# Batched matmul bound by its DMA queue: stores issued two at a time behind the loads of two groups, instead of one behind the loads of each group

## The chip, the cores and the metric

One core of a Trainium2 chip. The metric is the device time of one execution in microseconds, as the median of several runs. A program on one core has no second die to compare with, so the state of a single run can't always be told; all runs quoted here count as fast.

## The reference

```python
b1, b2, m, k, n = 8, 16, 256, 512, 384        # float32
def reference(x, weight):                      # (8,16,256,512) @ (8,16,512,384)
    return np.matmul(x, weight).astype(np.float32)
```

128 independent products. Per execution 167.8 MB are read and 50.3 MB are written.

## The kernel before

The batches go in 32 groups of four. Per group SP issues two weight loads (w, 1.57 MB each), one x load (2.10 MB) and, for an older group, one store (1.57 MB). VectorE casts w, ScalarE casts x and copies the products out of PSUM, TensorE makes 16 transposes and then 128 small matmuls. All DMAs go out from SP, so they form one queue on each of the 16 DMA engines.

```python
G, NG, T = 4, 32, 4            # batches in a group, groups, quarters of a group
XS, WS, OS = 2, 4, 4           # buffers of x_sb, w_sb, out_sb
LAG = 4
# ... cut
def load(e, t, U, s):                                     # group n = t * U + s
    for d in range(G // D):
        # waits until VectorE has cast what was in this w_sb slot (group n - 2)
        e.dma_start(w_sb[slot][:], ...).then_inc(w_in[slot], 16)
    # waits until ScalarE has cast x of group n - 2
    e.dma_start(x_sb[s % XS][:], ...).then_inc(x_in[s % XS], 16)

def store(e, t, U, s, pieces=1):
    # waits until ScalarE has copied group n out of PSUM
    e.dma_start(out=dram[:, rows], in_=out_sb[s % OS][:, rows]).then_inc(o_out[s % OS], 16)

def copy_out(e, t, U, s, q):
    if q == 0:
        # waits until store n - 4 has landed
    e.copy(out=out_sb[s % OS][:, 2 * q : 2 * q + 2, :], in_=po[...][:, :, :N])

def on_sync(e):
    U = OS
    for n in range(LAG):
        load(e, 0, NG, n)
    rounds = (NG - LAG) // U
    with e.Fori(0, rounds) as t:
        for s in range(U):
            load(e, t, U, LAG + s)
            store(e, t, U, s)
    for n in range(rounds * U, NG):          # the last four stores
        # ... cut
        store(e, 0, NG, n, T if n == NG - 1 else 1)
```

## Time and profile before

| | before |
|---|---|
| median | 518.28 us, 3 runs (518.17 to 518.58) |
| DMA queue | 218.11 MB, 99.3% of 16 engines' span |
| busiest compute engine | VectorE, 64% |
| landing of the last x load, first and last of 16 engines | 493.16 and 496.55 us |

A transfer lands on an engine when that engine raises the transfer's semaphore. The chart, the queue, the waits of SP and the windows of this kernel stand in the prediction. This is TensorE in order of time, around one group in mid-kernel (start us, length us, engine, line, what, count):

```profile
338.11 3.96 PE L166 MATMUL pt<-identity,x_bf 128*128 128x128 f32 x16 [5.47 <-ACT x_bf L132]
342.00 6.42 PE L180 MATMUL po<-w_bf,x_t 128*32 128x384 bf16 x128
```

The x load of this group landed on its last engine at 336.82 us. So TensorE's dense stretch (128 matmuls, each with a weight load) begins some 5 us after a group's x has landed; the store that stands next in the queue takes 3.6 us and is over by then. The other view is the end of the span, in windows of 5 us; the last two columns are the busy share of the DMA engines and GB/s:

```profile
500.00:505.00 5.00, 5.00 (x96) 3.52 (x99) 2.02 (x3) 2.02 (x3) 0.00 (x0) 0.88 1.01 428
505.00:510.00 5.00, 1.87 (x48) 1.01 (x40) 0.00 (x0) 1.72 (x3) 0.00 (x0) 1.00 0.98 409
510.00:515.00 5.00, 0.00 (x0) 0.00 (x0) 0.00 (x0) 0.00 (x0) 0.00 (x0) 0.64 0.44 177
```

The 16 engines don't finish together: in the last window some are done and others still write.

### The profile page before, as it was taken

What the parts mean: (1) busy time and instruction counts of PE and PEld (TensorE: products, weight loads), DVE (VectorE), ACT (ScalarE), POOL (GpSimd) and SP (SyncE); (2) the same over time, 40 slices, a digit from 0 to 9 for tenths busy, and PEclk for the clock granted to TensorE, in tenths of its full rate; (3) what the DMA queues carried; (4) which work ended last, traced back from release to release, by engine and by line L of the source; (5) the groups of instructions that cost most, each with busy time, mean ns of one, the idle gap of its engine ahead of it and who ended that gap; (6) DMA issues with size and microseconds to landing.
All of it is one profiled execution on the core that took longest, in us unless ns stands there. A gap on an engine that the chain in (4) does not pass through costs nothing.

```text
span 517.2 us, 11523 instructions
## 1 busy us (share of the span) xinstructions
PE 306.6 (59%) x4608; PEld 200.6 (39%) x4608; DVE 332.8 (64%) x384; ACT 236.7 (46%) x264; POOL 0.7 (0%) x6
## 2 busy tenths in 40 slices
PE   0478776556665457645577554776446765467752
PEld 0345444334443334433344332444324443244431
DVE  3698875667556676556675566855658656676550
ACT  0465564443644436435355354454444544544441
POOL 0000000000000000000000000000000000000000
PEclk9998877878777887878777778877788877778777
DMA  8999999999999999999999999999999999999996
GB/s 340 430 423 424 424 432 426 429 428 430 432 427 427 427 428 432 429 427 430 426 431 431 426 429 430 427 432 427 427 429 429 427 433 425 430 428 430 429 428 251
DMA packets 18869, 218.18 MB, mean 422 GB/s; under 512 B 2096, under 2 KB 2096, under 8 KB 2608
## 3 DMA queue, kind: packets, MB, share of 16 engines
q1 hardware_dynamic: 18864, 218.11, 99.3%
q8 instruction: 3, 0.05, 0.0%
q14 instruction: 2, 0.02, 0.0%
HBM read 167.77 MB, written 50.33 MB: 422 GB/s over the span
## 4 chain that ended last, share of the span: by engine, by line
DMA 81%; ACT 10%; PE 4%; issue 3%; ACTq 0%; SPq 0%
DMA x_sb<-in_x_dram 81%; ACT x_bf L132 9%; PE po L180 2%; PE pt L166 1%; ACTq L130 0%; ACT out_sb L194 0%; SPq L111 0%; SPq L103 0%; ACT L132 0%; ACTq L193 0%; SPq L282 0%; SPq L55 0%
## 5 line engine op out<-in xcount | busy, mean ns | idle before, releaser
L147 DVE CAST w_bf<-w_sb 64x1536 bf16<-64x1536 f32 x256 | 244.4, 955 | 47.2 <-DMA w_sb<-in_weight_dram 38.5
L166 PE MATMUL pt<-identity,x_bf 128*128 128x128 f32 x512 | 123.7, 425 | 199.3 <-ACT x_bf L132 199.1
L180 PE MATMUL po<-w_bf,x_t 128*32 128x384 bf16 x4096 | 185.1, 342 | 1.0 <-issue 1.0
L166 PEld LDWEIGHTS pt<-identity,x_bf 128*128 128x128 f32 x512 | 91.8, 216 | 232.1 <-issue 218.3
L194 ACT COPY out_sb<-po 128x768 f32<-128x768 f32 x128 | 102.2, 798 | 147.2 <-PE po L180 147.2
L153 DVE COPY x_t<-pt 128x1024 bf16<-128x1024 bf16 x128 | 88.4, 691 | 122.3 <-PE pt L166 121.8
L132 ACT CAST x_bf<-x_sb 128x1024 bf16<-128x1024 f32 x128 | 124.4, 1042 | 80.9 <-DMA x_sb<-in_x_dram 80.8
L180 PEld LDWEIGHTS po<-w_bf,x_t 128*32 128x32 bf16 x4096 | 108.8, 101 | 73.8 <-issue 14.2
L132 ACT ACT_TABLE_LOAD x8 | 10.3, 1283 | 42.9 <-DMA x_sb<-in_x_dram 42.9
masks.py:199 POOL TENSOR_SCALAR_AFFINE_SELECT identity<-identity 128x128 f32<-128x128 f32 x1 | 0.3, 292 | 0.2 <-POOL identity L200 0.2
L200 POOL MEMSET identity<- 128x128 f32 x1 | 0.2, 204 | 0.5 <-SPq L55 0.5
L271 POOL MEMSET const-bfloat16-1.0<- 128x1 bf16 x1 | 0.1, 101 | 0.0
L271 POOL MEMSET const-uint8-127<- 128x1 uint8 x1 | 0.1, 101 | 0.0
L271 POOL MEMSET const-float32-0.0<- 128x1 f32 x1 | 0.1, 98 | 0.2 <-issue 0.2
L271 POOL MEMSET const-float32-1.0<- 128x1 f32 x1 | 0.1, 98 | 0.0
## 6 DMA issues: line engine op xcount, KB each, us to landing
w_sb<-in_weight_dram SPq DMA_DIRECT2D x64, 1536.0 KB, 27.5
x_sb<-in_x_dram SPq DMA_DIRECT2D x32, 2048.0 KB, 27.5
out_dram<-out_sb SPq DMA_DIRECT2D x31, 1536.0 KB, 30.7
out_dram<-out_sb SPq DMA_DIRECT2D x4, 384.0 KB, 5.9
```

What stands on the lines that cost most here:

```text
L132: e.copy(out=x_bf[s % BS][:, rows], in_=x_sb[s % XS][:, rows].rearrange("p r (q s c) -> p r s q c", s=S, c=KO),).then_inc(x_cast, 1)
L147: e.tensor_copy(out=w_bf[(s * G + d * D + a) % WBS][h * HP : (h + 1) * HP], in_=w_sb[slot][a * HP : (a + 1) * HP, h * KO : (h + 1) * KO, : ...
L153: e.tensor_copy(out=x_t[s % TS][:, 2 * q : 2 * q + 2], in_=pt[(s * T + q) % PT][:].bitcast(bf16),).then_inc(t_copied, 1)
L166: ins = e.transpose(pt[(s * T + q) % PT][:, rr, h, :], words[:, 2 * q + rr, h :: KO // 2], identity[:],)
L180: ins = e.matmul(po[(s * T + q) % PO][mine, rr, :N], x_t[s % TS][:, 2 * q + rr, ko // 2, mine, ko % 2], w_bf[(s * G + i) % WBS][:, ko, :], ...
L194: e.copy(out=out_sb[s % OS][:, 2 * q : 2 * q + 2, :], in_=po[(s * T + q) % PO][:, :, :N],).then_inc(o_copied, 1)
L200: e.memset(identity[:], 0.0).then_inc(id_done, 1)
L271: nc = _bacc.Bacc("TRN2", target_bir_lowering=False, num_devices=1)
```

## The change

Its intent: the queue turns from loads to stores and back once for two groups rather than once for each.

```diff
-        for n in range(LAG):
+        for n in range(LAG + 1):
             load(e, 0, NG, n)
-        rounds = (NG - LAG) // U
+        store(e, 0, NG, 0)
+        load(e, 0, NG, LAG + 1)
+        store(e, 0, NG, 1)
+        store(e, 0, NG, 2)
+        first = LAG + 2
+        rounds = (NG - first) // U
         with e.Fori(0, rounds) as t:
-            for s in range(U):
-                load(e, t, U, LAG + s)
-                store(e, t, U, s)
+            for s in range(0, U, 2):
+                for a in range(2):
+                    load(e, t, U, first + s + a)
+                for a in range(2):
+                    store(e, t, U, first + s + a - LAG + 1)
(the loops over the last loads and stores, cut)
```

## The prediction

> **What bounds the kernel now.** I began with the page's chart of 40 slices and its table of DMA queues. One queue carries everything, and the DMA engines are over 90% busy in every slice but the first and the last, at 423 to 433 GB/s.
>
> ```profile
> DMA  8999999999999999999999999999999999999996
> GB/s 340 430 423 424 424 432 426 429 428 430 432 427 427 427 428 432 429 427 430 426 431 431 426 429 430 427 432 427 427 429 429 427 433 425 430 428 430 429 428 251
> q1 hardware_dynamic: 18864, 218.11, 99.3%
> ```
>
> No compute engine is near this: the busiest, VectorE, has 64% of the span. The chain that ended last is 81% the x load. So the time is bytes over rate, plus an edge at each end. The bytes don't change.
>
> Next the waits of the issuing engine (SP) and its instructions in order of time, to see whether the DMA engines ever run dry because an issue comes late.
>
> ```profile
> SPq L103 <- DVE w_bf L147: 269.5, 60, 8.6
> SPq L111 <- ACT x_bf L132: 122.5, 30, 5.6
> SPq L122 <- ACT out_sb L194: 35.5, 6, 16.2
> ...
> 205.23 4.29 SPq L103 DMA_DIRECT2D w_sb<-in_weight_dram  x2
> 213.89 0.33 SPq L111 DMA_DIRECT2D x_sb<-in_x_dram  x1
> 214.54 0.35 SPq L122 DMA_DIRECT2D out_dram<-out_sb  x1
> ...
> x_sb<-in_x_dram SPq DMA_DIRECT2D x32, 2048.0 KB, 27.5
> out_dram<-out_sb SPq DMA_DIRECT2D x31, 1536.0 KB, 30.7
> ```
>
> SP waits a lot, for casts that free w_sb and x_sb. But a load lands 27.5 us after its issue, and its own transfer takes under 5 us (2.10 MB at 429 GB/s), so some 22 us of other transfers stand ahead of it. The stores wait for their data in six places only, which lie at the end (the last group's pieces and those queued ahead of them).
>
> Third, the rate by stretch. The first group's store is issued at 46.74 us, and ring order puts it behind loads that land until about 64 us, so the first four windows are loads alone. The next three alternate one group of loads and one store. The last two begin after the last load is through on most engines: stores back to back.
>
> ```profile
> 5.00:17.00 12.00, 0.00 (x0) 0.00 (x0) 7.64 (x8) 0.00 (x0) 0.00 (x0) 1.00 1.01 429
> 17.00:29.00 12.00, 9.09 (x144) 6.21 (x144) 7.26 (x9) 7.58 (x9) 0.00 (x0) 1.00 1.00 428
> 29.00:41.00 12.00, 8.46 (x144) 5.46 (x144) 11.44 (x14) 6.98 (x9) 0.00 (x0) 1.00 1.01 427
> 41.00:53.00 12.00, 9.14 (x144) 5.93 (x144) 9.65 (x13) 7.49 (x9) 0.00 (x0) 0.86 1.01 426
> ...
> 132.00:164.00 32.00, 19.98 (x292) 13.38 (x292) 20.80 (x24) 15.63 (x19) 0.00 (x0) 0.77 1.01 428
> 200.00:264.00 64.00, 39.01 (x582) 25.39 (x584) 41.76 (x50) 29.60 (x33) 0.00 (x0) 0.79 1.01 429
> 300.00:364.00 64.00, 38.58 (x596) 25.45 (x584) 41.79 (x49) 30.44 (x35) 0.00 (x0) 0.79 1.01 429
> ...
> 497.00:500.00 3.00, 2.17 (x9) 1.73 (x10) 0.75 (x2) 3.00 (x4) 0.00 (x0) 0.50 1.01 430
> 500.00:503.00 3.00, 3.00 (x48) 2.16 (x51) 2.02 (x3) 0.55 (x1) 0.00 (x0) 0.81 1.01 430
> ```
>
> The last column is GB/s. Loads alone 426 to 429, alternating 428 to 429, stores alone 430. Changing direction twice per group costs nothing that shows.
>
> **What the Trainium skill says.** (1) "DMA: Bandwidth & Descriptors", section "Where 436 GB/s comes from", puts the ceiling of a core's 16 ports at 435.2 GB/s; here the steady windows hold 428 to 429, so 1.5% is all that any better order could reach. (2) The same page, "Anatomy of one DMA", says that DMA engines don't wait on semaphores; the wait sits on the issuing sequencer, and the engines just consume their queue. The trace agrees: SP's waits are in the hundreds of us while the queue is 99.3% busy. (3) Its section "Two DMAs through the same engine are not ordered" says that the read and the write sides of an engine are separate queues and that descriptors are pipelined. That would let a load's reads start while a store's writes finish, so a change of direction need not drain anything; the equal rates agree. (4) "HBM Reference", section "Latency", gives 0.2 us on average and 2 us under high load for an HBM access; no page I found gives a price for alternating reads and writes.
>
> **The change, part by part.**
>
> *Bytes, instructions, waits.* Nothing is added or removed: 96 loads, 35 store pieces, the same semaphore targets on each. Only SP's order changes. Before: load 4, store 0, load 5, store 1, and so on ("load" means a group's two w loads and its x load). After: loads 0 to 4, store 0, load 5, stores 1 and 2, then loads 6, 7, stores 3, 4, up to loads 30, 31, and stores 27 to 31.
>
> *Direction changes.* Before, stores 0 to 26 each stand alone among loads and 27 to 31 form the tail: 28 runs of stores. After: store 0, thirteen pairs, the same tail: 15 runs. So 26 changes of direction go. What is one worth? Count it from packets. In the trace's record of DMA packets the median 12,288-byte packet takes 460 ns and the median 16,384-byte packet 613 ns, the former also in the tail where all are stores. One group gives each of the 16 engines 16 w packets, 8 x packets and 8 store packets: 24 x 0.460 + 8 x 0.613 = 15.94 us. The measured period of a group, from the x issues at 213.89 and 277.49 four groups apart, is 63.60 / 4 = 15.90 us. Nothing is left over for switching; packets even overlap by some 0.04 us. The same by landings: in the loads-only stretch successive x loads land 12.26 us apart on most engines, and in the steady stretch groups are 15.88 us apart, so a store adds 3.62 us. In the tail, where store follows store, they land 3.61 to 3.63 us apart. Gain of 26 fewer changes: 0, at most 26 x 0.02 = 0.5 us.
>
> *The new issue order.* Does pairing make the queue run dry? Take T as the landing of the first x of a pair. The queue then serves w and x of the second group (x lands T+12.3), two stores (T+15.9, T+19.5), and the next w and x (T+31.8). SP can issue the next first x once the cast of this one is over, T+4 (four casts of 1.04 us), and it is needed at about T+27. The next second x waits for the cast of the group landing at T+12.3: cast over and issued by T+17, needed at T+39. Each has over 20 us in hand, as now. The pair of stores follows at once: ScalarE casts group k+1 only after it copied group k out, so by the time the second x may be issued both outputs are in out_sb. No store waits; half of them go out one group earlier than before, relative to the loads.
>
> *Buffers of out_sb.* Four; copying out group n needs store n-4 landed. The tighter store of a pair lands about 3.7 us behind the load of group n, and copying that group out begins some 6.5 us after its load (209.7 to 216.18). That is the margin of now, about 3 us; the other store of the pair gets one group more.
>
> *Compute in bursts.* Two groups now land 12.3 us apart, then 19.6 us pass. One group needs 11.2 us from its x landing to its last copy out (209.71 to 220.88), so it fits, and the loads-only opening already runs at that pace.
>
> *Tail.* The same five stores follow the last x load: no change. Sum: 518.28 + 0, less at most 0.5.
>
> **Rivals.**
>
> *Direction changes are dear and hidden in the 428 GB/s.* For it: it is the plain reason to write such a change, and the ceiling is 1.5% above. Against it: loads alone run no faster than the mixture. At its best it would take the kernel to the ceiling, 218.1 MB / 435.2 = 501 us plus some 8 us of edges: 509. I give this almost nothing.
>
> *Back-to-back stores slow the slowest engine.* The kernel ends with its slowest engine: of the 16 landings of each DMA the last comes 2.1 us after the first at the start and 3.4 us at the last x load. In the tail the last lander (taken to be one engine; the record doesn't name it) needed 3.75 us for the first store of the run, then 4.04 and 4.00 for the next two, with packets of up to 545 ns, while the others stayed at 3.6. If the second store of every pair costs it 0.29 us, thirteen pairs make 3.8 us: 522.1. Against it: the fourth store took 3.71 again, and loads after a pair may let it catch up. This is the likeliest way to lose, some 25%.
>
> *The lag shrinks.* In the steady stretch that engine loses under 0.1 us per group, on a few packets of 475 to 489 ns, all of 12,288 bytes. If alternation causes this, pairing halves it: about -1 to -1.5 us, 517.
>
> *A queue that runs dry, or copying out that waits for out_sb.* The margins above speak against both, and a late copy would eat slack of other engines first. Under 5%.
>
> **Range and chances.** Centre: mostly no change, with a small pull from the slow engine: 518.6. Low end 516.5 (the lag gone by half and a bit from switching), high end 521.8 (nearly the whole slow-engine cost). 2% is 10.4 us, beyond all but the first rival and an unforeseen stall: faster 0.01, same 0.97, slower 0.02.
>
> **What would show it.** In the changed profile: the DMA row at 9 throughout and steady windows at 428 to 430 GB/s; x landings alternating about 12.3 and 19.5 us apart; no store wait before the tail; four groups in 63.5 to 63.7 us. The second rival would show as a spread of landings beyond 4 us at the last x load and store packets above 500 ns in mid-kernel. I am wrong if the steady rate moves by over 3 GB/s, or if DMA slices fall below 9, with SP waiting for copies or casts longer than now.

## The result, and the profile after

The changed kernel takes 522.58 us in the median (522.34 to 522.69, 6 runs) against 518.43 us (518.17 to 518.58, 6 runs): 4.15 us or 0.8% slower, ratio 1.008 with a 95% interval of 1.0067 to 1.0093. Ratios here are the mean time of one kernel's fast runs over that of the other's of the same rounds, so not quite the ratio of the medians quoted. It is the same within 2%, as the odds had it, but above the range (516.5 to 521.8).

The chart, the queue and the waits of SP in the changed kernel:

```profile
DMA  8999999999999999999999999999999999999993
GB/s 344 431 426 426 413 431 427 429 430 429 426 430 426 429 432 425 430 425 429 431 429 432 429 425 427 428 431 424 431 429 427 432 428 426 428 428 431 426 426 159
q1 hardware_dynamic: 18864, 218.11, 98.8%
...
SPq L103 <- DVE w_bf L147: 306.2, 60, 9.4
SPq L111 <- ACT x_bf L132: 93.6, 30, 5.6
SPq L122 <- ACT out_sb L194: 37.0, 6, 19.7
```

Nothing went dry: the row is at 9 but for the edges, stores wait in the same six places, and the rate in mid-kernel is what it was. The clear difference is in the last slice, 159 GB/s where the kernel before had 251. The end in windows:

```profile
500.00:505.00 5.00, 3.38 (x16) 2.52 (x16) 3.60 (x5) 3.89 (x4) 0.00 (x0) 0.83 1.00 425
505.00:510.00 5.00, 5.00 (x105) 2.92 (x108) 0.69 (x1) 1.63 (x2) 0.00 (x0) 0.83 0.80 335
510.00:515.00 5.00, 1.25 (x32) 0.55 (x24) 0.00 (x0) 1.61 (x2) 0.00 (x0) 0.85 0.68 270
515.00:520.00 5.00, 0.00 (x0) 0.00 (x0) 0.00 (x0) 0.00 (x0) 0.00 (x0) 0.50 0.05 19
```

In the window from 505 us the engines are no longer all busy: most have done every transfer issued so far and wait for the last group's output, whose x load one of them completed late. The landings in the trace say how late. The trace holds 16 landings for each DMA, read here as one of each engine; the times of the first, the 15th and the last of them, for store 27, which follows the last x load:

```
                    first     15th      last
before              496.8     +2.60     +3.48 us
after               496.8     +3.37     +6.86 us
```

The first engine is where it was: 26 changes of direction fewer gained it nothing. The 15th is 0.8 us later, after stalls in the first 65 us that differ from run to run (e4 below has as much of them at store 1 and isn't slower). The last is 3.4 us later, and that is the whole difference of the two profiled runs (spans 517.2 and 520.6 us; the profiled run of the kernel before was a little longer than its median, so the medians differ by 4.15). In the second half of the changed kernel this spread grows with every pair of stores, from 3.34 us at the store that landed at 249.7 us to 6.75 us at the one of 475.5, seven pairs later: 0.49 us a pair. In the kernel before, the spread of x landings grows from 2.44 us (group 19, at 305.0 us) to 3.39 (group 31, twelve groups later): 0.08 us a group, 0.16 for two. The difference is 0.33 us a pair. For thirteen pairs that would be 4.3 us, an estimate from these stretches; measured are 3.4 us in the profiled runs and 4.15 in the medians.

Where does that engine lose it? The record of DMA packets, not a view of the page, gives every packet's length. Engines have no names in it; the late engine's packets are taken to be those that follow one another without a gap up to the last landing. Between an x landing at 338.63 and the end of the pair at 346.45 us these are over 473 ns (12,288 bytes each; the median of all is 460), beside what TensorE did:

```
first store     start 340.47 474   340.94 474   341.41 484   341.90 488      transposes
second store    start 342.38 485   342.86 474                                transposes
                start 343.33 502   343.83 516   344.34 540   344.88 512
                      345.39 521   345.91 500                                matmuls
```

TensorE in the changed kernel in order of time, over the same stretch:

```profile
342.91 0.74 PE L166 MATMUL pt<-identity,x_bf 128*128 128x128 f32 x4 [0.20 <-ACT x_bf L132]
...
343.58 5.38 PE L180 MATMUL po<-w_bf,x_t 128*32 128x384 bf16 x128
```

(One more of 479 ns, at 338.62, stands beside neither.) Packets of 500 ns and more come with the dense matmuls, which begin at 343.58. The same is seen at the end of the kernel before: after the first 20 us it has 13 packets of 12,288 bytes that took 495 to 600 ns, and all of them fall on dense matmuls. Ten follow one another from 501.7 to 506.9 us, and the last group's 128 matmuls run over the same time:

```profile
501.49 5.38 PE L180 MATMUL po<-w_bf,x_t 128*32 128x384 bf16 x128
```

So there are three theories, which the kernel before and the change alone don't tell apart.

- **Theory A:** one DMA engine moves store packets more slowly while TensorE runs matmuls. The change costs time because it moves the second store of each pair from before the matmuls into them.
- **Theory B** (the second rival of the prediction): the second of two stores in a row is slow on that engine, whatever runs beside it.
- **Theory C:** the change also moves half of the stores one group earlier; that place is what costs.

### The profile page after: what moved, and what is told of

It reads as the page before. It is cut to its first block, busy times and chain, and to the rows that moved or that the text cites. A ratio compares the mean times of both kernels' runs of the same rounds, so it can differ in the third digit from the quotient of the medians.

```text
span 520.6 us, 11473 instructions
## 1 busy us (share of the span) xinstructions
PE 294.8 (57%) x4608; PEld 193.9 (37%) x4608; DVE 332.1 (64%) x384; ACT 236.2 (45%) x264; POOL 0.7 (0%) x6
## 4 chain that ended last, share of the span: by engine, by line
DMA 80%; ACT 10%; issue 5%; PE 3%; ACTq 0%; SPq 0%
DMA x_sb<-in_x_dram 80%; ACT x_bf L132 9%; PE po L180 2%; PE pt L166 1%; ACTq L130 0%; ACT out_sb L194 0%; SPq L111 0%; SPq L103 0%; ACT L132 0%; ACTq L193 0%; SPq L289 0%; SPq L55 0%
## 5 line engine op out<-in xcount | busy, mean ns | idle before, releaser
L166 PE MATMUL pt<-identity,x_bf 128*128 128x128 f32 x512 | 116.7, 393 | 216.5 <-ACT x_bf L132 215.9
L180 PE MATMUL po<-w_bf,x_t 128*32 128x384 bf16 x4096 | 180.3, 336 | 0.0
L166 PEld LDWEIGHTS pt<-identity,x_bf 128*128 128x128 f32 x512 | 85.8, 214 | 249.0 <-issue 235.1
```

The costliest lines, as they stand in the source:

```text
L166: ins = e.transpose(pt[(s * T + q) % PT][:, rr, h, :], words[:, 2 * q + rr, h :: KO // 2], identity[:],)
L180: ins = e.matmul(po[(s * T + q) % PO][mine, rr, :N], x_t[s % TS][:, 2 * q + rr, ko // 2, mine, ko % 2], w_bf[(s * G + i) % WBS][:, ko, :], ...
```

## The experiments

All twelve are edits of the kernel before or of the changed one; their diffs are shortened here to the lines that matter. "Before" is the median of the kernel before in the same call, 518.5 to 518.6 us each time. The lag is that of the last engine behind the first at store 27, in the profiled run. Four chips: e1 to e4 on one, e5 to e8, e9 and e10, e11 and e12 on one each. The changed kernel itself was not timed again with them, so its 522.58 us are compared across calls.

| run | stores | TensorE | median us | ratio to before | lag us |
|---|---|---|---|---|---|
| before | single | full | 518.4 | 1 | 3.48 |
| after | pairs | full | 522.58 | 1.008 | 6.86 |
| e4 | single, one group earlier | full | 518.57 | 1.0000 | 3.36 |
| e1 | single, ahead of the x load | full | 530.62 | 1.0236 | 15.16 |
| e3 | single | quarter of the matmuls | 518.17 | 0.9994 | 3.09 |
| e2 | pairs | quarter of the matmuls | 520.40 | 1.0040 | 5.03 |
| e12 | single | nearly idle | 518.13 | 0.9994 | 2.88 |
| e11 | pairs | nearly idle | 518.89 | 1.0005 | 3.79 |
| e5 | single, x load in halves | full | 521.19 | 1.0052 | 3.18 |
| e7 | single between the halves | full | 526.53 | 1.0157 | 8.53 |
| e6 | pairs between the halves | full | 523.93 | 1.0103 | 6.20 |
| e10 | pairs, odd x loads cut 7 to 1 | full | 523.33 | 1.0098 | 6.55 |
| e9 | the same, pair ahead of the last eighth | full | 521.06 | 1.0047 | 4.75 |
| e8 | as e1, matmuls of half the columns | twice the instructions | 548.40 | 1.0567 | 20.93 |

### e4: single stores, one group earlier

```diff
-    LAG = 4
+    LAG = 3
```

> Single stores, but each one group earlier (behind the load of group n+3 instead of n+4), which is what the change did to half of the stores besides pairing them. Theories A and B: 518.4 us within 0.5. Theory C (the earlier place is what costs, 4 us for half of the stores): 526 us.

518.57 against 518.59 us (ratio 1.0, interval 0.9986 to 1.0014). Theory C falls: moving all stores one group earlier costs nothing.

### e1: single stores beside the matmuls

The store of a group stands between the w loads and the x load it had followed.

```diff
         for s in range(U):
-            load(e, t, U, LAG + s)
+            load(e, t, U, LAG + s)          # the two w loads alone
             store(e, t, U, s)
+            load_x(e, t, U, LAG + s)
```

> Single stores as in the kernel before, but each is put between the w loads and the x load of the group it follows, so that on every engine most of a store runs beside the previous group's matmuls. Theory A (one engine's store packets take about 520 ns instead of 462 while the matmuls run, single or paired): some 6 to 7 packets a store, 0.35 us x 27 stores, less the 2 us that this engine loses already: 524 to 528 us. Theory B (the second of two stores in a row is slow, whatever runs beside it): no store has another ahead of it, 518.4 us as before.

530.62 us, 12 us slower, above even the expected 524 to 528. No store follows another ahead of the tail, so B can't be the cause. The chart of this run's page, and its end in windows:

```profile
DMA  8999999999999999999999999999999999999943
GB/s 338 426 426 423 429 425 429 427 430 429 432 422 430 426 430 430 431 424 431 428 429 429 431 425 430 430 426 431 428 426 430 430 426 431 430 425 429 430 192 132
...
495.00:500.00 5.00, 3.36 (x15) 2.72 (x16) 1.69 (x3) 3.88 (x4) 0.00 (x0) 0.50 1.00 426
...
505.00:510.00 5.00, 0.72 (x20) 0.22 (x11) 3.90 (x5) 1.08 (x2) 0.00 (x0) 1.00 0.61 256
...
515.00:520.00 5.00, 5.00 (x85) 3.28 (x88) 2.08 (x3) 1.65 (x3) 0.00 (x0) 0.78 0.06 25
```

Full rate up to 500 us, then a long fall: in the window of 515 to 520 us 6% of the DMA engines' time is used, as much as one engine of 16. Its lag behind the first is 15.16 us at store 27, while the 15th engine's is 2.59, against 2.56 at store 1. So the other fifteen carry their stores beside the same matmuls and lose nothing. The packets over 475 ns that meet dense matmuls have a median of 526 ns.

### e3 and e2: a quarter of the matmuls, and e12 and e11: TensorE nearly idle

```diff
-                for ko in range(KO):
+                for ko in range(1):         # e2, e3: wrong result on purpose
```

> The changed kernel with a quarter of the matmuls (one block of K of four; wrong result on purpose). The matmul phase of a group shrinks from 5.3 to some 1.4 us, the order of the transfers stays. Theory A: the second store of a pair meets about a quarter of the slow packets, 518.5 to 520 us. Theory B: 522.5 us as with all matmuls.

> The kernel before with a quarter of the matmuls (wrong result on purpose), the control of the run above. Theory A: the tail loses its two slow stores (0.7 us), the small loss under transposes stays: 517.3 to 518.4 us. Theory B: the same as before, 518.4, or a little less because of the shorter last group.

The changed kernel falls from 522.6 to 520.40 us, the one before stays at 518.17. That is A's side, though 0.4 us above what it expected; 76 packets of some 484 ns remain, 61 of them beside transposes, and 26 of 495 to 600 ns, most of them at or next to the matmuls. So both were taken away, all but one transpose of each quarter of a group and one matmul of each quarter (4 of 16 and 4 of 128).

```diff
-            for rr in range(2):
-                for h in range(KO // 2):
+            for rr in range(1, 2):
+                for h in range(KO // 2 - 1, KO // 2):     # transposes
-            for rr in range(2):
-                for ko in range(KO):
-                    for i in range(G):
+            for rr in range(1, 2):
+                for ko in range(1):
+                    for i in range(G - 1, G):             # matmuls
```

> The changed kernel with one transpose and one matmul kept of every sixteenth of a group's TensorE work: 4 of 16 transposes stay in four places as 1 each, 4 of 128 matmuls (wrong result on purpose; PSUM is zeroed once at the start so that nothing unset is read). All transfers, casts and copies stay. Theory A: with TensorE nearly silent nothing slows the late engine, so pairing costs nothing: 516.8 to 518.4 us, within 0.7 us of its control, spread at the last x load 2 to 3 us. Theory B (the second store in a row): about 4 us above the control.

> The kernel before with the same cut of TensorE's work (wrong result on purpose), control of the run above. Both theories: 516.8 to 518.4 us; the loss under transposes and the two slow stores of the tail are gone, so the spread at the last x load stays at its opening 2.1 us.

518.89 and 518.13 us. Pairing, which costs 4.15 us beside a working TensorE, costs 0.76 us beside one that is nearly idle. Theory B would have left 4 us. The expectation of e11 was still missed, by 0.5 us and in its spread (3.66 us at the last x load), and the rest is no noise: the means differ by 0.70 us with a 95% interval of 0.35 to 1.06. It may be TensorE's as well. In e11, after the first 20 us, 49 packets of 12,288 bytes took 476 to 600 ns (in e12 there are 10), together 1.35 us more than 460 ns each would take, and all 49 overlap one of the instructions that were left, which only 42% of all such packets do. (On the chip of e11 and e12 no pair was run beside a full TensorE; on the three others the slow packets were there.)

The single-store control was expected at 2.1 us of spread at the last x load and has 2.83. One engine drifts without TensorE too: in e12 the 15th landing falls back from 1.36 us behind the first at store 11 to 2.59 at store 27, 0.08 us a group, as much as the last one does in the kernel before. The cause of this drift is open.

### e5, e7 and e6: stores between the halves of an x load

These were meant as the way out: if the matmuls are over 10.4 us after a landing, a store put later than that should be undisturbed. The x load is issued as two halves, and e7 puts the single store, e6 the pair, between them.

```diff
             load(e, t, U, LAG + s)                 # w
-            load_x(...); store(e, t, U, s)         # in the kernel before, in words
+            load_x(e, t, U, LAG + s, 0)
+            store(e, t, U, s)                      # e7, e6 (a pair); e5: behind both halves
+            load_x(e, t, U, LAG + s, 1)
```

> Each x load is issued as two halves of 1 MB, one behind the other; the stores stay where the kernel before has them. It is the control of the next two runs. Every theory: 518.5 us within 0.7; a price of splitting would show here.

> Single stores as in the kernel before, each between the two halves of an x load, 9.8 to 13.4 us after the previous landing, when the matmuls are over. Theory A: even the small loss of the kernel before (stores beside transposes, some 0.07 us a group) goes, 516.5 to 518 us; the spread of landings at the last x load stays near 2.2 us where before it was 3.4. Theory B: 518.5 us as the control.

> Stores in pairs as in the changed kernel, but each pair stands between the two halves of the second group's x load, some 13 to 20 us after the first group's load landed and so after its matmuls, which end at about 10.4 us. Theory A (the slow packets come from running beside the matmuls): paired stores cost nothing here, 516.5 to 518.5 us, and no run of packets over 500 ns before the tail. Theory B (second store in a row): 522.5 us.

All three missed. The control already costs 2.6 us for 32 DMAs more, 0.08 us each. But the halves are also moved in twice as many packets, of 8,192 bytes, with a median of 312 ns where one of 16,384 takes 613. That is 11 ns more for each of the 256 packets that an engine had for x, 2.8 us together (an estimate), so the packets alone may explain it. And e7 and e6 are slower still, 526.53 and 523.93 us, because the placing was wrong: I took the distance from landing to the end of the matmuls as 10.4 us, from one group without an activation-table load ahead of its cast (1.28 us on ScalarE where it stands). In the run of e7 a group landed at 393.78 us on its last engine and its dense matmuls ran from 400.24 to 405.62, so until 11.8 us after it; store packets of 492 to 540 ns follow one another from 403.1 to 405.7. The packets of these runs speak for theory A: of those of 495 to 600 ns, all 105 in e7 and all 74 in e6 overlap dense matmuls. One pair of e6 even turns theory B round. Its x piece landed on the late engine at 402.51, the first store at 406.46 and the second at 410.15 us: 3.95 us for the first, 3.69 for the second. There the first was the one beside the matmuls, which ran from 398.79 to 404.17.

### e9 and e10: the pair moved by an eighth of one x load

With the lesson from e7: the x load of each odd group is cut 7 to 1. In e10 the pair follows both pieces, as the change has it; in e9 it stands ahead of the small one. The two differ in the place of that piece only.

```diff
 load_x(e, t, U, first + s + 1, 0)                 # seven eighths
-load_x(e, t, U, first + s + 1, 1)                 # e10: here
 for a in range(2):
     store(e, t, U, first + s + a - LAG + 1)
+load_x(e, t, U, first + s + 1, 1)                 # e9: here
```

> Pairs as in the changed kernel, with the x load of every odd group cut 7 to 1 (1.75 MB and 0.25 MB) and the pair between the two pieces. On the last engine both stores then run from about 11.7 us after the previous landing up to just before the next, when no matmul runs (in the two runs with halves the store began 9.2 us after it and still met the matmuls, which on the chip lasted until 11.8). Theory A: no packets over 495 ns from the pairs; the spread of landings stays near 3 us; 518.4 us plus up to 1.6 us for 16 more DMAs: 518.5 to 520.3 us. Theory B (second store in a row): 522.5 plus the same 1.6: 524 us.

> The control: the same cut of the x loads, but the pair behind both pieces, as the changed kernel has it. Nothing differs from the run above but that the 0.25 MB piece goes ahead of the pair, which sets the landing, and with it the matmuls, 7.3 us earlier against the stores. Theories A and B: 522.5 plus up to 1.6 us: 522.5 to 524.2 us.

521.06 against 523.33 us: moving a quarter of a megabyte from before the pair to behind it takes 2.3 us off. Direction as A said, size short of it (the expectation ended at 520.3): packets above 500 ns are still there, at 401.8 to 403.4 us for instance, under the end of a group's matmuls. A group inside a pair has the next one only 12.3 us behind it, so its matmuls end close to the pair. The control e10 came out as expected. In e9 the late engine isn't alone: the 15th landing is 4.52 us behind the first at store 27, nearly as late as the last, and of its 59 packets of 495 to 600 ns 22 stand beside no TensorE instruction, most of them several at the same time (at 86.4 and 182.1 us for instance). Their cause is open, so part of what e9 still costs isn't explained by theory A.

### e8: twice the TensorE instructions

```diff
+for c in range(2):
+    cols = slice(c * N // 2, (c + 1) * N // 2)
     for ko in range(KO):
         for i in range(G):
-            ins = e.matmul(po[...][mine, rr, :N], x_t[...], w_bf[...][:, ko, :], ...)
+            ins = e.matmul(po[...][mine, rr, cols], x_t[...], w_bf[...][:, ko, cols], ...)
```

> The order of the first run (stores beside the matmuls, 530.6 us), with each matmul cut into two of half the columns (right result): twice the PE instructions for the same moving data. If the slowing of that engine's store packets goes with the PE instructions per us and these double: packets of some 600 ns instead of 530, about 545 us. If it goes with the data that PE reads: packets stay near 530 ns, 530 to 533 us. If PE can't issue twice as fast, its matmul phase doubles instead and nothing is told apart but that all 8 packets of a store are slow (533 us).

548.40 us. TensorE does issue twice as fast: windows of 5 us inside a dense stretch, e1 first and e8 second. The count in the first pair of brackets is matmuls, in the second weight loads.

```profile
386.00:391.00 5.00, 5.00 (x112) 3.01 (x108) 4.84 (x6) 1.90 (x3) 0.00 (x0) 0.86 1.01 427
```

```profile
211.00:216.00 5.00, 5.00 (x244) 5.00 (x240) 4.84 (x6) 2.41 (x3) 0.00 (x0) 0.98 1.01 424
```

The late engine's store packets beside dense matmuls go from a median of 526 ns to one of 606: over the usual 460 that is 66 and 146 ns, a little more than double. The moving data is the same in both. So the slowing goes with the number of TensorE instructions per microsecond, or with their weight loads, which double as well, and not with the columns that are streamed. (The total is more than this alone: from about 330 us on the rate falls, in most slices to 330 to 400 GB/s, and slow packets stand beside no matmul too. The likely reason, not tested, is that with the late engine up to 20 us behind the others run out of issued work.) Transposes, 16 in 3.96 us where matmuls are 128 in 5.38, give packets of some 484 ns. Each of them loads 128 x 128 float32 as weights where a matmul loads 128 x 32 bfloat16, so weight bytes would have ordered the two the other way round; that argues for the count of instructions, without showing it.

### A version that beats both

None was found. The kernel before already has each store behind the x load and ahead of the dense matmuls: it has 13 packets of 495 to 600 ns, and of the other orders beside a full TensorE only e4, which equals it in time, has as few (11). With TensorE all but idle it takes 518.13 us (e12), so what this effect leaves to be gained there is under 0.1%.

## Why the prediction was right or wrong, point by point

- **The bound, and that the queue wouldn't run dry: right.** The rate in mid-kernel and the waits of stores are what they were, and on the first engine x landings alternate by 12.3 and 19.5 us as worked out.
- **"Gain of 26 fewer changes: 0, at most 0.5 us": right.** The first engine reaches store 27 at 496.8 us in both kernels. With TensorE nearly idle, pairing gains nothing either (e11, e12).
- **Sum "518.28 + 0": wrong, and this is the step that failed.** The working asked of each new place of a store only whether data, buffers and issue were ready, and took a packet's 460 ns as fixed wherever it stands. It isn't fixed on one engine of 16: beside dense matmuls a store packet over 473 ns takes 512 ns in the median (changed kernel). So that engine loses 0.33 us more with each pair than with two single stores, and as the slowest of the 16 it ends the kernel: 522.58 us. The view that would have told it was at hand. In the tail of the kernel before, the slow packets begin and end with the last group's matmuls.
- **The second rival: right in size, wrong in cause, and given too little weight.** It named the engine, the sign (a spread beyond 4 us, packets above 500 ns) and 522.1 us; measured were 522.58. But being second in a row isn't the cause (e1: no pairs and 12 us; e6: a pair whose second store is the fast one; e11: 0.76 us is left at most). Its term, 0.29 us a pair, is 0.33 against the kernel before. The hope that "loads after a pair may let it catch up" failed: the lag grew up to the last pair, and a queue at 9 in every slice leaves no slack in which to catch up. So that 522.1 came near the measured time was partly luck: the size was read from two stores of the tail that were slow for the same reason, and the reason given was another.
- **"The fourth store took 3.71 again" as evidence against it: misread.** It was fast because the matmuls were over at 506.9 us.
- **"The lag shrinks": wrong.** Pairing doesn't lessen the small loss of the kernel before. Nor does that loss need TensorE's work, as I had also thought: it goes on at 0.08 us a group with TensorE nearly idle (e12).
- **The range:** its high end was set just under the whole cost of the second rival, with 25% given to it. It should have contained it.

Shown by runs: that TensorE's work beside the stores makes most of the cost, 3.4 of 4.15 us (e11 and e12; e1 and e2 agree), and that neither pairing alone nor the earlier place does (e1, e4, e11). Open: whether the last 0.76 us are its too, why it is one engine, which one (the landings carry no names), whether instructions or weight loads do it, and by what path.

## What to carry to other kernels

In a kernel bound by the DMA queue, the time is that of the slowest of 16 engines, and the mean rate hides it: look at the spread of landings and at the fall of the rate in the last slices. When transfers are reordered, ask for each one not only what it waits for but what runs beside it in its new place, and compare packet lengths under busy and idle compute. Orders can be compared cheaply with an experiment that silences the compute and leaves all transfers in place.

## What the Trainium skill lacked or had wrong

- "SBUF — State Buffer", section "SBUF: two separate sides", says "A DMA cannot be slowed by a compute op, and vice versa." Here store packets issued from SP take 526 ns beside dense matmuls and 606 ns beside twice as many, against 460 otherwise, on one engine of 16; with TensorE nearly idle 3.4 of the 4.15 us that pairing costs are gone. Whether the meeting place is SBUF the runs don't say.
- "DMA: Bandwidth & Descriptors", section "Latency and other measured facts", knows of DMA engines that are usually slower and suspects descriptor rings that GpSimd's queue uses. Here no DMA comes from GpSimd, and one engine is slower all the same, in its stores: up to 15.16 us behind the first at store 27, where the 15th is 2.59 behind.
- No page found gives a price for alternating reads and writes in one queue. Here it is nil: with 26 changes of direction fewer the first engine lands store 27 at 496.8 us in both kernels.
